# Filling the expert gate matrices by accumulating scatters into zeroed DRAM instead of one-hot products

## The chip, the core and the metric

One core of a Trainium2 chip runs the kernel. The metric is the device time of one execution in microseconds. Its engines are TensorE (PE, with its weight loads PEld), VectorE (DVE), ScalarE (ACT), GpSimd (POOL) and SyncE (SP), which here issues nearly all plain DMAs; POOL issues the indirect ones. All DMAs share 16 transfer engines.

## What is computed

A backbone of two layers over 512 latent and 256 context tokens of width 1024: gated DeltaNet in layer 0, attention in layer 1, each followed by a retrieval of experts (PEER). Everything is float32. The part that matters:

```python
def block_fn(xb):                                  # 128 tokens
    qry = (xb @ w_query).reshape(P, PEER_HEADS, 2, PEER_HALF)
    s = jnp.einsum('phcd,hckd->phck', qry, sub_keys)
    top_s, top_i = lax.top_k(s, PEER_TOPK)
    ...
    best_s, pos = lax.top_k(cand_s, PEER_TOPK)     # 16 of 256 pairs, for each of 8 heads
    idx = jnp.take_along_axis(cand_i, pos, axis=-1)   # expert 0..16383
    gate = jax.nn.softmax(best_s, axis=-1)
    act = jax.nn.gelu(jnp.einsum('pd,phkd->phk', xb, u_tab[idx]), approximate=False)
    coef = gate * act
    return jnp.einsum('phk,phkd->pd', coef, v_tab[idx])
```

So a token has 128 picks among 16384 experts, and one expert may be picked by several heads.

## The kernel before

The latents are four blocks of 128 tokens, the context two. For `ND` = 3 latent blocks the experts are evaluated densely, all 16384 for all 384 tokens; for latent block 3 and, in layer 0, for the context, the picked rows of `peer_u` and `peer_v` are gathered from DRAM by indirect DMAs, 128 rows of 4 KB each.

The dense way goes over 128 blocks of 128 experts. `act(i)` loads 512 KB of U (tile `ur`), splits it into a high and a low part (`uh` on ACT, `ul` on DVE) and makes 24 matmuls into `up` and a gelu: an act block. `mix` loads 512 KB of V (`vr`), splits it, multiplies the gelu by the gates, and makes 18 matmuls into six accumulators `y`: a mix. Some act blocks are done ahead of the dense loop, beside earlier stages, and go through DRAM (`act_d`, 192 KB each way); `tock` hands them out by the table `URATE`, as `tick` hands out steps of the gathers by `RATE`.

The mix needs the gates as a matrix [expert, token]. `gates_build` makes it after `routing`: for every token two one-hot 128x128 tiles A and B on DVE (lines 1066 and 1067), whose product on PE (`gp`, line 1068) is the token's 128x128 gate matrix; ACT copies four tokens at a time into `st` (line 1069). Five groups of 64 tokens are stored to DRAM (`G_d`, 4 MB each, line 1071) and read back 640 KB at a time in the dense loop (`gt`); the sixth stays in SBUF.

Stages, by the profile's time: dn_in and DeltaNet of context and latents; routing of layer 0 to 1950 us; gates 1950 to 2322; dense loop 2332 to 3184; attention to 3541; routing of layer 1; gates 3792 to 4105; dense loop 4112 to 4872. Block 3 is routed first, then 0, 1 and 2. The background gathers of layer 0 run through all of it: `gather_u` (line 965, a DVE product for each gathered row, line 967), `gather_v` for the context (line 1017, two matmuls on PE into `yp` for each gathered tile, line 1020) and `gather_vt` (line 981). A gather needs a free `row` buffer, and DVE or PE frees it.

A scheduler orders the instructions of each engine when the program is built; the program text sets only what depends on what. An engine runs its instructions in that order and stops at one that has to wait. On SP's and on POOL's queue each DMA also waits for the eighth one before it.

At the start SP loads the conditioning weights, then the first `dn_w_in` weights (`wr`), the tokens (`xt`, lines 288) and the modulation rows `modg`, `modS`, `modA` (one row of 4 KB spread over 128 partitions); the first normalized row (`hrow`) needs these.

Of the kernel before, what the change touches and what calls it, by code (L numbers as in the profile page):

```python
# [18 lines left out]
P = 128  # L19
# [12 lines left out]
AHEAD = [i for r in (0, 2, 1, 3) for i in range(r, PK, 4)]      # blocks of experts, in the order of their evaluation ahead  # L32


class Kern:
    def __init__(self, ctx, tc, I, out, dbg):
# [3 lines left out]
        self.ug, self.ucredit, self.nu = None, 0.0, 0  # L40
        self.cst = ctx.enter_context(tc.tile_pool(name="cst", bufs=1))
# [7 lines left out]
        nc.vector.memset(self.ones, 1.0)  # L49
        self.nhalf = c.tile([P, 64], F32, name="nhalf")  # L50
# [3 lines left out]
    # gathers are issued in small steps between the other work  # L54
# [18 lines left out]

    def drain(self, keep=0):
        while len(self.bg) > keep:
            for _ in self.bg.pop(0):
                pass
        self.credit = 0.0
# [43 lines left out]
    def ada(self, l, r, pool=None):  # L122
        """chunks 2 * r and 2 * r + 1 of a layer's modulations, for latents (row 0) and context (row 1)"""
# [24 lines left out]
    def mod_rows(self, pool, l, s, sub, norm, nb=1, pool_g=None, **kw):  # L148
        """A = norm_g*(1+scale), S = shift, as rows on all partitions"""
# [10 lines left out]
    def norm_mod(self, pool, x, A, S, h):  # L160
        """h <- rmsnorm(x) * A + S"""
# [8 lines left out]
    def transp_split(self, pp, tag, h, hi, lo, b):  # L170
        """h [128, 1024] -> hi/lo[:, kb, b*128:...]"""
# [10 lines left out]
    # tokens on the free axis: 0..511 latents, 512..767 context  # L182
    def gate_math(self, p, pp, gx, n, G):
# [23 lines left out]
        # log1p(e) = ln(u) * e / (u - 1), or e where u rounds to 1  # L207
# [30 lines left out]
    def dn_in(self, G, later, ast, rec):  # L238
        """q, k, v, z and the gates; rec's first step is traced before the last heads, beside which it runs"""
# [67 lines left out]
    def dn_qkv(self, G, p, pp, pwp, hi, lo, wtile, heads, nb):  # L307
# [4 lines left out]
        W2 = TL + 4 + TC          # conv output span: latents, gap of 4, context  # L312
        XC = TL + 6               # start of the context in the padded row
# [28 lines left out]
        for h in heads:  # L342
# [80 lines left out]
    def dn_rec(self, seq, G, og_d, st_d):  # L423
# [5 lines left out]
        with ExitStack() as st:  # L429
# [8 lines left out]
            for g0 in range(0, QH, GR):  # L438
                pks, Pss, Us = [], [], []
                pg = p if g0 // GR % 2 else pq  # L440
                for hh in range(GR):
                    h = g0 + hh
                    Ps = pg.tile([P, MH, 2, P], F32, name="Pm", bufs=GR)
                    U = pg.tile([P, MH, 2, P], F32, name="U", bufs=GR)     # (c, v), dir
# [5 lines left out]
                    for c in range(n):  # L450
# [124 lines left out]
    def dn_inv(self, p, pp, Us, MH, Z64):  # L575
        """Us[head][:, m, dir] <- (I + U)^-1, U triangular (upper for dir 0, lower for dir 1)."""
# [23 lines left out]
        R1 = t4("R1", [P, 2 * M, 32])     # rows of the inverses' transposes  # L600
        R2 = t4("R2", [P, 2 * M, 32])     # rows of the inverses
# [9 lines left out]
        # (source, target) blocks  # L611
# [56 lines left out]
    def dn_out(self, seq, og_d, xin, xout, put):  # L668
        """xout[b] = xin[b] + g1 * (o @ w_out); put(b, rows) for every finished block"""
# [33 lines left out]
    def attention(self, xl, xc, order, rows, A0, gst, ost, pst):  # L703
        """(softmax(q k^T) v)^T of the latents, split, by heads; context is read after the gathers that finish it"""
# [3 lines left out]
        with tc.tile_pool(name="att", bufs=1) as p:  # L708
# [95 lines left out]
            with tc.tile_pool(name="att3", bufs=1) as p, tc.tile_pool(name="attp", bufs=1, space=PS) as pp:  # L804
                sc = P ** -0.5
                H2 = N * P // 2
                for h in range(QH):
# [28 lines left out]
                    nc.sync.dma_start(wr, I["att_w_out"][h * P:(h + 1) * P, :])  # L836
                    self.split(wh[:, h], wl[:, h], wr)
# [24 lines left out]
    def routing(self, l, hi, lo, T, gate, idx, order, done=None):  # L862
        """gate[b], idx[b]: [128 tokens, 8 heads, 16]"""
        nc, I = self.nc, self.I
        n = T // P
        with self.tc.tile_pool(name="rt", bufs=1) as q, self.tc.tile_pool(name="rtp", bufs=1, space=PS) as pp:
# [32 lines left out]
            for b in order:  # L899
# [17 lines left out]
                for h in range(PH):  # L917
                    self.tick(self.rate[3])
                    self.tock(1)
# [34 lines left out]
                if done:  # L954
                    done(b)
# [79 lines left out]
    def gates_build(self, l, tbs, gate, idx, G_d, pk):  # L1035
# [3 lines left out]
        with tc.tile_pool(name="gb", bufs=1) as p, tc.tile_pool(name="gbp", bufs=1, space=PS) as pp:  # L1039
            iota = p.tile([P, P], F32, name="iotar")  # L1040
            nc.sync.dma_start(iota, self.I["iota128"].to_broadcast([P, P]))
            for b in tbs:
# [8 lines left out]
                for j in range(3):  # L1051
                    nc.tensor.transpose(tp[:, j], f3[:, j], self.ident)
# [390 lines left out]
```

## Time and profile before

| | |
|---|---|
| median of 3 runs | 4889.07 us (4887.17 to 4899.61) |
| the profiled execution's span | 4891.1 us |
| PE, DVE, ACT, POOL busy | 4329.9, 3587.0, 1866.5, 1321.5 us |
| DMA | 1196.55 MB, mean 245 GB/s |
| POOL's indirect DMAs | 1024 |

A row of busy time by stretch gives the stretch from the span's start, its length, the busy time of PE, PEld, DVE, ACT and POOL, each with its instructions (x), TensorE's granted clock as a share of full, the mean busy share of the 16 DMA engines and what they moved. A row in order of time gives the start, the duration, the engine (SPq is SP's queue), the line, the operation with out<-in, the count, and in brackets the engine's idle time before it and what ended it. An indirect DMA's duration on POOL is that of its issue, not of the transfer.

### The profile page before, as it was taken

Reading aid. Unit: us, or ns where it says so; the run is one execution under the profiler, and the core shown is the slowest. Engines: PE = TensorE matmul, PEld = TensorE weight load, DVE = VectorE, ACT = ScalarE, POOL = GpSimd, SP = SyncE. Lnnn points to the kernel's source line nnn. Section 1 sums busy time; section 2 is a strip of 40 time slices with the busy share of each in tenths; the row PEclk is TensorE's granted clock in tenths of the full one; section 3 lists DMA queues with packets and bytes.
Section 4 is the critical chain, followed back from the end, with each engine's and each line's share of the span. In section 5 each row is a group of like instructions: output and inputs, shape, how many; then the busy total and the mean of one; then the engine's idle time right before and its main releaser. Section 6 shows DMA issues by size and latency. Waiting matters only on the chain. (4 is left out here: it accounts for less than half of the span.)

```text
span 4891.1 us, 68996 instructions
## 1 busy us (share of the span) xinstructions
PE 4329.9 (89%) x24564; PEld 3455.1 (71%) x24564; DVE 3587.0 (73%) x8483; ACT 1866.5 (38%) x3605; POOL 1321.5 (27%) x1111
## 2 busy tenths in 40 slices
PE   6999669757569698999999999988997999999998
PEld 3778547545444556666788888745687998888887
DVE  4667825899965857566688888645579888888886
ACT  2335553447450213344333333223333554333333
POOL 0000000134344433222333334440000102444441
PEclk8999789768679899999999999999999999999999
DMA  7744246447578877777999999872133678999996
GB/s 296 261 150 135 75 144 191 153 148 254 177 242 317 301 240 268 269 260 272 329 349 351 339 339 337 292 268 74 61 112 107 215 260 287 355 334 335 336 324 230
DMA packets 480616, 1196.55 MB, mean 245 GB/s; under 512 B 40752, under 2 KB 239152, under 8 KB 470416
## 3 DMA queue, kind: packets, MB, share of 16 engines
q1 hardware_dynamic: 332816, 655.21, 38.2%
q0 software_dynamic: 147456, 536.94, 31.5%
q8 instruction: 194, 3.18, 0.3%
q14 instruction: 150, 1.23, 0.1%
HBM read 1079.50 MB, written 112.49 MB: 244 GB/s over the span
## 5 line engine op out<-in xcount | busy, mean ns | idle before, releaser
L965 POOL DMA_INDIRECT row<-in_peer_u,idx x512 | 613.2, 1198 | 1513.3 <-DVE row L967 706.3
L100 PE MATMUL up<-hil,uh 128*128 128x384 f32 x2048 | 709.4, 346 | 44.7 <-ACT c L1094 44.1
L102 PE MATMUL up<-hil,ul 128*128 128x384 f32 x2048 | 697.2, 340 | 0.0
L101 PE MATMUL up<-lol,uh 128*128 128x384 f32 x2048 | 696.1, 340 | 0.0
L100 PE MATMUL y<-vh,ch 128*128 128x512 f32 x1536 | 602.8, 393 | 9.1 <-ACT ch L106 7.6
L101 PE MATMUL y<-vl,ch 128*128 128x512 f32 x1536 | 602.9, 393 | 0.0
L102 PE MATMUL y<-vh,cl 128*128 128x512 f32 x1536 | 508.8, 391 | 0.0
L981 POOL DMA_INDIRECT row<-in_peer_v,idx x256 | 339.9, 1328 | 456.3 <-DVE lhs L984 374.5
L100 PEld LDWEIGHTS up<-hil,uh 128*128 128x128 f32 x2048 | 386.9, 189 | 94.8 <-ACT c L1094 65.4
L106 ACT CAST uh<-ur 128x1024 fp32r<-128x1024 f32 x256 | 268.3, 1048 | 454.3 <-PE up L101 322.3
L1017 POOL DMA_INDIRECT row<-in_peer_v,iT x256 | 279.5, 1092 | 557.7 <-PE yp L1020 473.7
L107 DVE TENSOR_TENSOR vl<-vr,vh 128x1024 fp32r<-128x1024 f32 x256 | 312.9, 1224 | 127.1 <-ACT vh L106 125.1
L106 ACT CAST vh<-vr 128x1024 fp32r<-128x1024 f32 x256 | 268.6, 1051 | 359.9 <-PE y L102 325.0
L101 PEld LDWEIGHTS up<-lol,uh 128*128 128x128 f32 x2048 | 387.1, 189 | 19.2 <-issue 10.9
L102 PEld LDWEIGHTS up<-hil,ul 128*128 128x128 f32 x2048 | 386.5, 189 | 18.2 <-issue 15.1
L107 DVE TENSOR_TENSOR ul<-ur,uh 128x1024 fp32r<-128x1024 f32 x256 | 312.1, 1220 | 74.7 <-ACT uh L106 70.1
L967 DVE SCALAR_TENSOR_TENSOR row<-row,ghs 128x1024 f32<-128x1024 f32 x256 | 311.2, 1222 | 73.7 <-DMA row<-in_peer_u,idx 72.7
L1066 DVE TENSOR_SCALAR A<-iotar,kt 128x128 f32<-128x128 f32 x768 | 221.8, 289 | 174.4 <-PE gp L1068 171.9
L100 PEld LDWEIGHTS y<-vh,ch 128*128 128x128 f32 x1536 | 289.8, 189 | 70.3 <-ACT ch L106 9.1
L102 PEld LDWEIGHTS y<-vh,cl 128*128 128x128 f32 x1536 | 288.6, 188 | 64.6 <-issue 4.2
L984 DVE SCALAR_TENSOR_TENSOR lhs<-row,lcf,lhs 128x1024 f32<-128x1024 f32 x254 | 325.1, 1280 | 9.6 <-DMA row<-in_peer_v,idx 8.0
L101 PEld LDWEIGHTS y<-vl,ch 128*128 128x128 f32 x1536 | 290.1, 189 | 56.3 <-issue 2.5
(397 smaller groups left out, 8788.1 us busy)
## 6 DMA issues: line engine op xcount, KB each, us to landing
ur<-in_uT SPq DMA_DIRECT2D x256, 512.0 KB
vr<-in_peer_v SPq DMA_DIRECT2D x256, 512.0 KB
w<-in_ada_w SPq DMA_DIRECT2D x48, 1024.0 KB
G_d<-st SPq DMA_DIRECT2D x10, 4096.0 KB
gt<-G_d SPq DMA_DIRECT2D x64, 640.0 KB
act_d<-c SPq DMA_DIRECT2D x129, 192.0 KB
c<-act_d SPq DMA_DIRECT2D x129, 192.0 KB
wr<-in_dn_w_in SPq DMA_DIRECT2D x48, 512.0 KB
```

Of the source, the lines that this page charges most:

```text
L100: first = mm(ps, lh, rh, start=start, stop=False)
L101: mm(ps, lh, rl, start=False, stop=False)
L102: mm(ps, ll, rh, start=False, stop=stop)
L106: self.nc.scalar.copy(hi, src)
L107: self.nc.vector.tensor_sub(lo, src, hi)
L965: nc.gpsimd.indirect_dma_start(out=u, out_offset=None, in_=self.I["peer_u"], in_offset=bass.IndirectOffsetOnAxis(ap=ix[:, k:k + 1], axis=0))
L967: mv = nc.vector.scalar_tensor_tensor(u, u, 1.0, hs, op0=ALU.mult, op1=ALU.mult, accum_out=coef[:, k:k + 1])
L981: nc.gpsimd.indirect_dma_start(out=v, out_offset=None, in_=self.I["peer_v"], in_offset=bass.IndirectOffsetOnAxis(ap=ix[:, k:k + 1], axis=0))
L984: keep(nc.vector.scalar_tensor_tensor(y, v, coef[:, k:k + 1], y, op0=ALU.mult, op1=ALU.add))
L1017: nc.gpsimd.indirect_dma_start(out=v, out_offset=None, in_=self.I["peer_v"], in_offset=bass.IndirectOffsetOnAxis(ap=iT[:, t:t + 1], axis=0))
L1066: nc.vector.tensor_scalar(A, iota, kt[:, 0, t:t + 1], None, op0=ALU.is_equal)
```

## The change

`gates_build` is gone. In its place stand six matrices in DRAM, `Gd[layer][block]`, each [16384 experts x 128 tokens], 8 MB, addressed as (j, i, token) for expert i * 128 + j. `zeros` splits each into eight pieces of 16 rows of 64 KB, and `fill` writes three of them from a DRAM row of zeros after every head of `dn_qkv` and of the attention. `places` computes each pick's address (four DVE operations for a block); `gates_place` issues for each of a block's 128 picks one indirect DMA on POOL that adds 128 gates, one for each token, into the matrix. `scat` takes a step of each block in turn, one step for each head in `routing` and the rest in `place_all`, which also calls `tick` and `tock`. The dense loop reads the gates of four expert blocks with three DMAs of 256 KB, and multiplies once instead of twice. The rates change: `RATE[0][4]` 0.88 to 0.3, `RATE[0][7]` 2.6 to 1.6, layer 0's `URATE` 0.07 and 15 to 0.2 and 2, layer 1's 0.33 to 0.23, with two small ones in layer 1.

```diff
+    def scat(self, w):
+        self.scredit += w
+        while self.scredit >= 1.0:
+            self.scredit -= 1.0
...
+            try:
+                next(self.todo[self.turn])
+                self.turn += 1
+            except StopIteration:
+                self.todo.pop(self.turn)
+
+    def fill(self, n):
+        for _ in range(min(n, len(self.fills))):
+            dst = self.fills.pop(0)
+            self.nc.sync.dma_start(dst, self.I["zero"].to_broadcast(list(dst.shape)))
...
             nc.sync.dma_start(self.pk_d[h], pk.rearrange("p a b c -> p (a b c)"))
+            self.fill(ZF)
...
-                            nc.vector.tensor_scalar(A, iota, kt[:, 0, t:t + 1], None, op0=ALU.is_equal)
-                            nc.vector.tensor_scalar(B, iota, kt[:, 1, t:t + 1], kt[:, 2, t:t + 1], op0=ALU.is_equal, op1=ALU.mult)
-                            nc.tensor.matmul(ps[:, j], B, A, start=True, stop=True)
-                        nc.scalar.copy(st[:, :, q * 4:q * 4 + 4].rearrange("p i t -> p t i"), ps)
-                    if g < G_d.shape[0]:
-                        nc.sync.dma_start(G_d[g], st.rearrange("p i t -> p (i t)"))
...
+    def gates_place(self, G, gate, at):
+
+        for k in range(PH * TOPK):
+            self.nc.gpsimd.indirect_dma_start(out=G, out_offset=bass.IndirectOffsetOnAxis(ap=at[:, k:k + 1], axis=0),
+                                              in_=gate[:, k:k + 1], in_offset=None, compute_op=ALU.add)
+            yield
...
-                nc.vector.tensor_mul(c1, c1, gt)
-                nc.vector.tensor_mul(c[:, T1:], c[:, T1:], gl[:, i])
...
+                    gt = p.tile([P, nb, GS, P], F32, name="gt", bufs=3)
+                    for b in range(nb):
+                        nc.sync.dma_start(gt[:, b].rearrange("p i t -> p (i t)"), G[b].rearrange("(j x) o -> j (x o)", j=PK)[:, i * P:(i + GS) * P])
...
+    def place_all():
+        while k.todo:
+            k.tick(k.rate[4])
+            k.tock(2)
+            k.scat(1.0)
+
+    def zeros(l):
+        k.fills += [g.rearrange("(j x) o -> j (x o)", j=PK)[j:j + 16] for g in Gd[l] for j in range(0, PK, 16)]
```

How the change moves instructions is shown at three places. The first is SP at the start, from the first `wr` loads on; this is before:

```order
L253 DMA wr<-in_dn_w_in 128x8x128 x2
L288 DMA xt<-in_x 128x1024 x2
L143 DMA ada_d_68<-row 2x512 x2
L154 DMA modg<-in_norm_g 128x1024
L143 DMA ada_d_68<-row 2x512 x2
L154 DMA modg<-in_norm_g 128x1024
L316 DMA cw<-in_convw 128x160
L146 DMA modS<-ada_d_68 128x1024 x2
L253 DMA wr<-in_dn_w_in 128x8x128
L146 DMA modA<-ada_d_68 128x1024 x2
L288 DMA xt<-in_x 128x1024 x2
L288 DMA xt<-in_ctx 128x1024 x2
```

After, eighteen fills (of the matrices numbered 85, 86 and 87, layer 0's) follow the first two `wr` loads, then two `xt` loads and the conditioning rows; the next rows there are these (88 to 90 are layer 1's matrices):

```order
L340 DMA cw<-in_convw 128x160
L277 DMA wr<-in_dn_w_in 128x8x128
L161 DMA bt<-in_ada_b 1x512 x8
L277 DMA wr<-in_dn_w_in 128x8x128
L96 DMA G_87<-in_zero 16x16384 x6
L96 DMA G_88<-in_zero 16x16384 x8
L96 DMA G_89<-in_zero 16x16384 x8
L96 DMA G_90<-in_zero 16x16384 x8
L170 DMA modS<-ada_d_70 128x1024 x2
L170 DMA modA<-ada_d_70 128x1024 x2
L312 DMA xt<-in_x 128x1024 x2
L312 DMA xt<-in_ctx 128x1024 x2
```

All 48 fills now stand ahead of the modS and modA rows and of the last four token loads.

The second is POOL in layer 0, where the gathers of the context's values end and those of `gather_u` for latent block 3 follow, beside the gates; before, with the semaphores waited for:

```order
L1017 DMA row_17463<-in_peer_v,iT_16047 128x1024 [waits DMASW3_49,PE_49]
L1017 DMA row_17489<-in_peer_v,iT_16047 128x1024 [waits DMASW4_49,PE_49]
L965 DMA row_17543<-in_peer_u,idx03_90 128x1024 [waits DMASW5_49,PE_49]
L965 DMA row_17568<-in_peer_u,idx03_90 128x1024 [waits DMASW6_49,PE_49]
L965 DMA row_17615<-in_peer_u,idx03_90 128x1024 [waits DMASW7_49,PE_49]
L965 DMA row_17640<-in_peer_u,idx03_90 128x1024 [waits DVE_49]
L965 DMA row_17665<-in_peer_u,idx03_90 128x1024 [waits DVE_49]
L965 DMA row_17690<-in_peer_u,idx03_90 128x1024 [waits DVE_49]
```

After, at the end of the same `gather_u` stretch (G00, G01 and G02 are layer 0's matrices, lg and la a block's gates and addresses):

```order
L992 DMA row_20327<-in_peer_u,idx03_97 128x1024 [waits DMASW7_49,DVE_49]
L992 DMA row_20361<-in_peer_u,idx03_97 128x1024 [waits DVE_49]
L1065 DMA G02_87<-lg2_13614,la2_13620 2097152x1 [waits DMASW3_49,DMASW1_49]
L1065 DMA G00_85<-lg0_13612,la0_13618 2097152x1 [waits DMASW5_49,DMASW2_49]
L1065 DMA G01_86<-lg1_13613,la1_13619 2097152x1 [waits DMASW6_49]
L1065 DMA G02_87<-lg2_13614,la2_13620 2097152x1 [waits DMASW4_49,DMASW1_49]
L1065 DMA G00_85<-lg0_13612,la0_13618 2097152x1 [waits DMASW2_49]
L1065 DMA G01_86<-lg1_13613,la1_13619 2097152x1 [waits DMASW3_49]
L1065 DMA G02_87<-lg2_13614,la2_13620 2097152x1 [waits DMASW7_49,DMASW4_49]
L1065 DMA G00_85<-lg0_13612,la0_13618 2097152x1 [waits DMASW5_49,DMASW0_49]
```

From there 151 scatters follow one another with no gather between, each waiting for a queue's semaphore (DMASW) of a DMA before it. In the whole of layer 0's placing POOL has 148 scatters among 116 context gathers, then 85 among 96 gathers of `gather_u`, then the 151; in layer 1 384 scatters among 91 gathers, the first 80 of them alone.

The third is PE in layer 0 up to the first mix; before:

```order
L1068 MATMUL gp<-A,B 128x128 x3
L1020 MATMUL yp<-row,Cz 32x512 x2
L1068 MATMUL gp<-A,B 128x128 x4
L1020 MATMUL yp<-row,Cz 32x512 x2
L1068 MATMUL gp<-A,B 128x128 x3
L1020 MATMUL yp<-row,Cz 32x512 x8
L100 MATMUL y_20097<-vh,ch 128x512
L101 MATMUL y_20097<-vl,ch 128x512
```

After:

```order
L124 MATMUL up<-hil,uh 128x384
L125 MATMUL up<-lol,uh 128x384
L126 MATMUL up<-hil,ul 128x384
L124 MATMUL y_20309<-vh,ch 128x512
L125 MATMUL y_20309<-vl,ch 128x512
L124 MATMUL y_20310<-vh,ch 128x512
L125 MATMUL y_20310<-vl,ch 128x512
```

The products `gp` are gone from PE; where 59 act blocks stood ahead of the first mix, 112 do now (in layer 1 73 and 124).

## Rows read from the trace of the kernel before

**Rows 1.** the page: span and part 1, busy time and instructions of each engine
```profile
span 4891.1 us, 68996 instructions
PE 4329.9 (89%) x24564; PEld 3455.1 (71%) x24564; DVE 3587.0 (73%) x8483; ACT 1866.5 (38%) x3605; POOL 1321.5 (27%) x1111
```

**Rows 2.** busy by stretch: PE, PEld, DVE, ACT, POOL; clock, DMA share, GB/s
```profile
1917.00:2332.00 415.00, 389.14 (x2163) 271.34 (x2161) 255.20 (x849) 157.47 (x185) 121.70 (x115) 0.98 0.78 271
2332.00:3184.00 852.00, 849.62 (x4062) 726.57 (x4062) 672.28 (x975) 295.03 (x396) 330.80 (x282) 1.00 0.92 334
3758.00:4112.00 354.00, 333.52 (x2135) 326.66 (x2133) 300.26 (x919) 177.80 (x221) 37.97 (x32) 1.00 0.65 227
4112.00:4872.00 760.00, 758.93 (x3622) 666.81 (x3623) 622.66 (x893) 273.49 (x366) 314.02 (x225) 1.00 0.91 327
```

**Rows 3.** groups by line, shapes: busy us, mean ns, idle before and its releasers
```profile
L1067 DVE TENSOR_SCALAR B<-iotar,kt 128x128 f32<-128x128 f32 x768 | 264.1, 344 | 0.0
...
L1068 PE MATMUL gp<-A,B 128*128 128x128 f32 x1536 | 224.5, 283 | 2.7 <-ACT st L1069 2.5
...
L1066 DVE TENSOR_SCALAR A<-iotar,kt 128x128 f32<-128x128 f32 x768 | 221.8, 289 | 174.4 <-PE gp L1068 171.9 <-PE up L102 1.3 <-PE up L101 0.4
```

**Rows 4.** PE in order of time: start, us, engine, line, operation
```profile
2041.73 1.05 PE L1020 MATMUL yp<-row,Cz 128*32 128x512 f32 x4
2042.71 1.38 PE L1068 MATMUL gp<-A,B 128*128 128x128 f32 x10
...
2046.08 0.34 PE L100 MATMUL up<-hil,uh 128*128 128x384 f32 x1
...
2047.64 0.34 PE L100 MATMUL up<-hil,uh 128*128 128x384 f32 x1
...
2601.31 0.40 PE L100 MATMUL y<-vh,ch 128*128 128x512 f32 x1
...
2604.08 1.52 PE L102 MATMUL y<-vh,cl 128*128 128x512 f32 x6
```

**Rows 5.** SP's DMA issues at the start
```profile
37.23 1.02 SPq L146 DMA_DIRECT2D modA<-ada_d  x2
...
39.67 1.28 SPq L288 DMA_DIRECT2D xt<-in_ctx  x2
```

**Rows 6.** PE at the start, in order of time
```profile
51.77 1.94 PE L176 MATMUL tr<-ident,hrow 128*128 128x128 f32 x8 [22.79 <-DVE hrow L302]
```

**Rows 7.** busy by stretch, of the start and of one gate store
```profile
27.00:60.00 33.00, 8.96 (x44) 3.82 (x44) 18.57 (x25) 11.28 (x19) 6.25 (x8) 0.52 0.91 338
...
2044.00:2068.00 24.00, 19.06 (x99) 14.17 (x99) 9.66 (x35) 6.95 (x9) 2.93 (x4) 0.86 0.94 347
```

**Rows 8.** POOL in order of time, gathers of gather_u
```profile
1275.23 0.93 POOL L965 DMA_INDIRECT row<-in_peer_u,idx  x1 [1.35 <-DVE row L967]
...
1278.95 1.18 POOL L965 DMA_INDIRECT row<-in_peer_u,idx  x1 [0.30 <-issue]
...
1481.68 0.95 POOL L965 DMA_INDIRECT row<-in_peer_u,idx  x1 [1.07 <-DVE row L967]
```

**Rows 9.** DVE in order of time, the products of two of these gathers
```profile
1280.35 1.23 DVE L967 SCALAR_TENSOR_TENSOR row<-row,ghs 128x1024 f32<-128x1024 f32 x1 [1.02 <-DMA row<-in_peer_u,idx]
...
1489.33 1.22 DVE L967 SCALAR_TENSOR_TENSOR row<-row,ghs 128x1024 f32<-128x1024 f32 x1 [0.72 <-DMA row<-in_peer_u,idx]
```

**Rows 10.** DVE: block 0's indices cast, layer 0 and layer 1
```profile
1914.70 0.22 DVE L946 CAST li<-idf 128x128 int32<-128x128 f32 x1
...
3756.86 0.22 DVE L946 CAST li<-idf 128x128 int32<-128x128 f32 x1
```

**Rows 11.** PE: the first mix of layer 0 and of layer 1
```profile
2332.45 0.80 PE L100 MATMUL y<-vh,ch 128*128 128x512 f32 x1 [1.43 <-issue]
...
4112.15 0.80 PE L100 MATMUL y<-vh,ch 128*128 128x512 f32 x1 [6.50 <-ACT ch L106]
```

**Rows 12.** SP: one plain DMA issue
```profile
2044.80 0.32 SPq L1071 DMA_DIRECT2D G_d<-st  x1
```

More of the change, by code (lines that the diff above doesn't have):

```diff
@@ L954, in routing @@
                 if done:
-                    done(b)
+                    done(q, b)
     def gather_u(self, l, p, hs, gate, idx, coef):
@@ L1099, in act_ahead, with dense @@
         self.nc.sync.dma_start(self.act_d[i], c)
-    def dense(self, G_d, gl, xin, put, rp=None):
+    def dense(self, G, xin, put, rp=None):
         nc, tc, I = self.nc, self.tc, self.I
@@ L1250, in body @@
     k.act_d = dr("act_d", [PK, P, ND * P])
-    G_d = dr("G_d", [ND * 2 - 1, P, PK * 64])
+    Gd = [[dr(f"G{l}{b}", [PK * PK * P, 1]) for b in range(ND)] for l in range(2)]
     pers = ctx.enter_context(tc.tile_pool(name="pers", bufs=1))
@@ L1258, in picks, with place @@
         p = st.enter_context(tc.tile_pool(name="lgi", bufs=1, side="right"))
-        return [{b: p.tile([P, PH, TOPK], t, name=f"{nm}{b}") for b in range(ND)} | of(d, 0) for d, nm, t in ((gate, "lg", F32), (idx, "li", I32))]
+        lat = [{b: p.tile([P, PH, TOPK], t, name=f"{nm}{b}") for b in range(ND)} | of(d, 0) for d, nm, t in ((gate, "lg", F32), (idx, "li", I32))]
+        return lat, {b: p.tile([P, P], I32, name=f"la{b}") for b in range(ND)}
+    def place(l, q, b, lat, at):
+        k.places(q, lat[1][b], at[b])
+        k.todo.append(k.gates_place(Gd[l][b], lat[0][b].rearrange("p h k -> p (h k)"), at[b]))
+    def place_all():
[5 more added lines that the diff above has]
+        k.fills += [g.rearrange("(j x) o -> j (x o)", j=PK)[j:j + 16] for g in Gd[l] for j in range(0, PK, 16)]
     of = lambda d, s: {b: v for (q, b), v in d.items() if q == s}
@@ L1274, in body @@
         rec = k.dn_rec("c", G, og_c, st_d)
+        zeros(0)
         k.dn_in(G, [k.ada(l, r) for l in range(2) for r in range(3) if l or r], st, rec)
@@ L1314, in body, with gathers @@
         vctx(i // 2, i % 2)
-    def gathers(b):
-        if b >= ND:
+    def gathers(q, b):
+        if b < ND:
+            place(0, q, b, lat, at)
+        else:
             j = NX + b - ND
@@ L1332, in put @@
         fresh.pop(b - 2, None)
-    gl = k.gates_build(0, range(ND), *lat, G_d, lst.enter_context(tc.tile_pool(name="gk", bufs=1)))
+    place_all()
     k.tock(3)
@@ L1339, in body @@
     A0 = k.mod_rows(ap, 1, 0, 0, "norm1_g", pool_g=k.up, tag="raw", bufs=3)
-    k.dense(G_d, gl, xm_l, put, ap)
+    k.dense(Gd[0], xm_l, put, ap)
     lst.close()
@@ L1353, in body @@
     k.drain(2 * NX - NVA)
+    zeros(1)
     k.attention(xo_l, xo_c, [*range(ND, NL), *range(1, ND), 0], fresh, A0, gst, ost, pst)
@@ L1371, in body, with gathers @@
     k.dense_open(lst, 1, ND, hi, lo)
-    def gathers(b):
-        if b >= ND:
+    def gathers(q, b):
+        if b < ND:
+            place(1, q, b, lat, at)
+        else:
             gat.u(1, b - ND, gate[0, b], idx[0, b])
             gat.v(b - ND, idx[0, b], (1, 0, 5), rows(xm2, b), lambda y: put(b, y))
-    lat = picks(gst)
+    lat, at = picks(gst)
     k.routing(1, hi, lo, TL, *lat, order, gathers)
-    gl = k.gates_build(1, range(ND), *lat, G_d, lst.enter_context(tc.tile_pool(name="gk", bufs=1)))
+    place_all()
     k.tock(3)
-    k.dense(G_d, gl, xm2, put)
+    k.dense(Gd[1], xm2, put)
     k.drain()
```

69 lines of the change are left out of this document (26 added, 43 removed).

## The prediction

> **What bounds the kernel now.** I read the page first, then busy time by stage, then PE's, POOL's and SP's order of time in the stages that the change touches. Sums are made against the profiled execution, 4891 us [rows 1], 2 us over the median of the three runs. PE is busy for 89% of it. The two gate stages and the two dense stages fill it almost wholly [rows 2]: from layer 0's first ready indices to its first mix PE works 389 of 415 us, in layer 1 334 of 354; in the dense stages 850 of 852 and 759 of 760, beside DMA at 0.92 and 0.91 of its time and 334 and 327 GB/s. So DVE's one-hot products (222 and 264 us for both layers, 225 us of PE with them [rows 3]) do not stand in the way by themselves: act blocks fill the gaps beside them. What the change can win is PE's share of the products, about 225 us, and only if PE has other work throughout.
>
> PE's prices: nine `up` matmuls start in 1.56 us, so an act block of 24 is 4.2 us; twelve `y` matmuls in 2.77, so a mix of 18 is 4.15; one gathered context value is 0.98 [rows 4]. Layer 1's dense stage confirms it: 55 acts and 128 mixes are 231 + 531 = 762 us against 760.
>
> **Part 1: the zeros.** 48 fills of 1,048,576 bytes are 50.3 MB, DRAM to DRAM. The code writes three per head of dn_in and of the attention; but nothing holds them, and in SP's order all 48, layer 1's too, stand between the first two `wr` loads and the modS, modA, x and ctx loads. In the trace these are issued at 37 and 40 us [rows 5], and PE's first transpose, which had waited 22.8 us for the normalized row, comes at 51.8 [rows 6]. All of dn_in is behind that, so the fills' whole time lies on the path. Nothing hides it: the stretch from 27 to 60 us already has DMA at 0.91 and 338 GB/s [rows 7]. No row shows a DRAM to DRAM copy. From below: a stretch with a 4 MB store to DRAM moves 347 GB/s [rows 7], so 145 us. From above: each byte is read from DRAM and written to it, which no row has; both counted at 347 GB/s give 290 us. A gain is excluded, since nothing was there before. No row is nearer to one end, so I take the middle: **+217**. The fills' source is one row read over and over; the rows of [rows 7] hold such broadcast loads and are not slow, so I add nothing for that. The Trainium skill (DMA: Bandwidth & Descriptors, Latency and other measured facts) gives copies between HBM tensors 207 GB/s at a row pitch of 512 KiB and 103 at 4 MiB; an estimate from the first is 243 us, and the sum would be 5536. No run here shows such a copy.
>
> **Part 2: placing in layer 0.** 384 scatters of 128 elements replace the products. Each goes to one of three matrices and waits until the one before it on the same matrix has landed; POOL issues in order, so behind a waiting scatter stand the gathers, behind these DVE's row products, and behind those DVE's `ul` splits, on which PE's act blocks wait. I call three scatters, one per matrix, a round. A POOL issue takes 0.93 to 0.95 us and 0.30 more to the next [rows 8], so I take 1.25 per DMA, a scatter's 128 descriptors like a gather's. How long a scatter takes to land no row shows. The nearest row is a gather: issued at 1275.23, its DVE product starts at 1280.35, a wait that the row ended: 5.1 us; in a saturated stretch it is 1481.68 to 1489.33, 7.65 [rows 8, 9]. A scatter moves almost nothing, but reads DRAM before it writes there. Ends: 3.75 us a round (POOL's own three issues) and 7.5; I take 5.0 beside act blocks, next to the 5.1, and 4.5 where acts have run out. The Trainium skill (DMA: Bandwidth & Descriptors, Anatomy of one DMA) gives a fixed 2.0 us plus bytes over 436 GB/s. By that the gather would be 0.93 + 3.2 = 4.1 us, where the row shows 5.1; a round would fall to POOL's three issues, which is the first rival below.
>
> Block 0's indices are cast at 1914.7 [rows 10]; with the address arithmetic the first scatter stands at 1917 in the old clock. POOL's order has three stretches. (a) 148 scatters among 116 context gathers: POOL 264 x 1.25 = 330; PE's order has 52 acts there, 52 x 4.2 + 116 x 0.98 = 332. Each waits for the other at times: 340. (b) 85 scatters among 96 gathers for `gather_u`: 181 x 1.25 = 226, PE's 38 acts (160) beside them. (c) 151 scatters with nothing between, 53 rounds with the last matrix's lag: 53 x 4.5 = 239; PE has done the 112 acts that its order puts ahead of the first mix, and idles. Sum 805. SP's `gt` loads wait for the last scatters too, and all later `vr` and `ur` loads are queued behind them. 8 us for that load put the first mix at 2730, 398 later than 2332 [rows 11].
>
> In return, 16 acts instead of 69 are left. PE: 16 x 4.2 + 128 x 4.15 + 37 context values x 0.98 = 634 us. But DMA has V 67.1 MB, U 8.4, stored acts 22.0, gates 25.2 and 197 gathers 103.3, together 226 MB; at 340 GB/s, between the dense stages' 334 and the 347, that is 664, which decides. The stage ends at 3394 against 3184: **+210**. That 15 of the context values leave the attention's start I count at nothing (at most 15 us). The fewer DVE instructions of a mix (one product instead of two) lie under it too.
>
> **Part 3: placing in layer 1.** First scatter at 3757 [rows 10]. Twelve scatters go to matrix 0 before matrix 2's first, so the last chain ends after about 139 rounds. With 91 gathers among 384 scatters POOL's own issues are 475 x 1.25 = 594; 139 rounds of 5.0 are 695, and the waits decide. PE's 107 acts (449) fit beside. First mix at 3757 + 695 + 8 = 4460 instead of 4112 [rows 11]. Then 4 acts and 128 mixes are 548 us of PE, but V 67.1, U 2.1, acts 24.4, gates 25.2 and 165 gathers 86.5 MB are 205 MB, 604 us at 340 GB/s. End 5064, and the 19 us from 4872 to the span's end as before: 5083, **+192**.
>
> Sum: 4891 + 217 + 210 + 192 = **5510**. Setting up addresses (four small DVE operations a block) and the removed 4 MB stores (42 MB, against 50 MB of gate loads and 50 of zeros) are inside the stages above.
>
> **Rivals.** *The scatter lands fast*, and POOL's three issues set a round. For it: it carries 512 bytes; against: the 5.1 us. (a) 340, (b) 226, (c) 53 x 3.75 = 199: first mix 2690, end 3354, +170. Layer 1: 594, end 4982, +91. With the same fills **5369**.
>
> *The scatter lands slowly*, 7.5 us, as gathers in a saturated stretch do, because each element is read before it is written and shares its queue with gathers. (a) 49 rounds 368, (b) 28 rounds 230, (c) 53 x 7.5 = 398: first mix 2921, end 3585, +401; layer 1: 139 x 7.5 = 1043, end 5431, +540. **6049**.
>
> *PE alone sets the pace from the first scatter to the last mix* (the other side). Place: both placings and dense stages. Layer 0 then takes 332 + 160 + 8 + 634 us and ends at 3051, -133; layer 1 takes 449 + 8 + 548 and ends at 4781, -110; with the fills **4865**. It decides from a round of 3.2 us among layer 1's gathers (449 / 139) and of 0.5 us in stretch (c) ((4891 - 4865) / 53), so from scatters that cost POOL less than the 0.32 us that a plain issue costs SP [rows 12], against 0.93 [rows 8]; and DMA would have to carry 205 MB in 548 us, 374 GB/s, where no stretch shows over 347.
>
> That the change does not do what it says holds for the fills alone: they are not early beside other work but ahead of it, as costed.
>
> **How the numbers follow.** Forecast 0.50, fast landing 0.24, slow landing 0.20, PE's pace 0.04, something else between 0.02. The predicted time is the forecast's, 5510. With fills at 145 the fast case is 5297, and DMA some per cent faster takes it to 5180; with fills at 290 the forecast is 5583, and landings between 5.0 and 7.5 reach 6000. The range 5180 to 6000 leaves out PE's pace, the end of the fast case and the upper half of the slow one, about 2 in 10. A measurement of this kernel tells 0.3% from no change. Faster by more needs PE's pace: 0.04. Within 0.3%: 0.02. Slower: 0.94.
>
> **What would show it.** Part 1: PE idle and DMA near full from about 30 to 245 us, then dn_in as before; wrong if the stretch is under 100 us or other work stands in it. Part 2: PE idle in layer 0 for some 240 us before its first mix while POOL issues nothing but scatters, each wait ended by the scatter before on its matrix; wrong if PE stays busy there. Part 3: rounds of about 5 us on POOL in layer 1, `y` starting some 350 us after the old 4112 plus the shift already gathered. Dense: DMA over 0.9 busy and PE below 0.95. The forecast falls if scatters land in under 4 us or over 6, or if a scatter's own POOL time is far from 0.95.

## The result, and the profile after

The changed kernel takes **5993.9 us** (median of 4 runs, 5991.4 to 5999.3) beside 4891.2 for the kernel before on the same chip (4887.2 to 4899.6): a ratio of 1.225, 95% interval 1.2235 to 1.2269. That is inside the range, at its upper edge, and 484 us above the forecast of 5510.

The page of the profiled execution, its span, part 1 and three rows of the slices (each slice 150 us), answering to [rows 1]:

```profile
span 5997.5 us, 65797 instructions
PE 4324.0 (72%) x23010; PEld 3373.9 (56%) x23010; DVE 3216.6 (54%) x6691; ACT 1661.2 (28%) x3407; POOL 2580.0 (43%) x1879
PE   0599769575679987767007999988974655559998
POOL 0000000143453378888884344300038888843332
PEclk5799889676789998898558999989997787879999
```

PE lost its products and is still busy for 4.3 ms: the granted clock of the whole execution fell from 0.933 to 0.862 of full, and the matmuls into `up` of one line take 375 ns on average instead of 346. POOL's busy time nearly doubled. PE is at zero in the slices 1, 20 and 21, and where POOL stands at 8, PE stands at 4 to 7 or at 0.

Busy time by stretch, answering to [rows 2, 7] (PE, PEld, DVE, ACT, POOL, granted clock, DMA share, GB/s): the fills, the three parts of layer 0 (placing beside other work, scatters alone, dense), then layer 1 (placing, the time to the first mix, dense).

```profile
60.00:120.00 60.00, 0.00 (x0) 0.00 (x0) 0.24 (x1) 0.00 (x0) 0.00 (x0) 0.50 0.95 300
...
2103.00:2895.00 792.00, 573.10 (x2658) 434.96 (x2656) 243.68 (x309) 132.29 (x183) 649.80 (x452) 0.88 0.81 231
2895.00:3168.00 273.00, 0.00 (x0) 0.00 (x0) 0.00 (x0) 0.00 (x0) 224.32 (x146) 0.50 0.25 6
3182.00:3846.00 664.00, 646.33 (x2860) 502.71 (x2860) 491.25 (x604) 211.98 (x289) 262.77 (x205) 1.00 0.94 342
...
4408.00:5327.00 919.00, 512.35 (x2323) 468.18 (x2323) 243.49 (x303) 139.19 (x194) 736.94 (x476) 0.81 0.59 128
5327.00:5403.00 76.00, 46.83 (x230) 43.63 (x228) 23.10 (x28) 15.51 (x22) 12.31 (x12) 0.88 0.69 231
5403.00:5981.00 578.00, 548.92 (x2400) 448.99 (x2400) 468.38 (x578) 193.19 (x264) 205.01 (x154) 1.00 0.92 340
```

POOL's busy time does not hold the 0.30 us between two issues. With it POOL is full: 650 + 452 x 0.30 = 785 of 792 us, and 737 + 476 x 0.30 = 880 of 919. It is the bound of both placings. Its instructions in order of time, first where scatters run alone in layer 0, then beside gathers in layer 1, answering to [rows 8]:

```profile
2962.29 1.55 POOL L1065 DMA_INDIRECT G<-lg,la  x1 [0.30 <-issue]
2964.15 1.55 POOL L1065 DMA_INDIRECT G<-lg,la  x1 [0.30 <-issue]
2966.01 1.55 POOL L1065 DMA_INDIRECT G<-lg,la  x1 [0.30 <-issue]
...
4804.19 1.55 POOL L1065 DMA_INDIRECT G<-lg,la  x1 [0.30 <-issue]
4806.05 0.99 POOL L992 DMA_INDIRECT row<-in_peer_u,idx  x1 [0.30 <-issue]
4807.35 1.58 POOL L1065 DMA_INDIRECT G<-lg,la  x1 [0.30 <-issue]
...
4840.45 1.98 POOL L1065 DMA_INDIRECT G<-lg,la  x1 [0.30 <-issue]
```

A scatter's issue is 1.55 us, not the gather's 0.95, and the idle time before it ends by the issue itself, not by an earlier scatter. Three scatters, one per matrix, are 5.57 us, longer than a landing (a median of 3.4 us, shown further on), so the landing is mostly hidden. The scatters of layer 1's placing as a group (busy, mean ns, idle before, and what ended it), then its last scatter, and PE's first mix in layer 0 and in layer 1:

```profile
L1065 POOL DMA_INDIRECT G<-lg,la x383 | 637.7, 1665 | 372.8 <-DVE idf L972 221.1 <-issue 108.1 <-DMA G<-lg,la 43.7
...
5324.30 1.57 POOL L1065 DMA_INDIRECT G<-lg,la  x1 [1.76 <-DMA G<-lg,la]
...
3182.48 0.79 PE L124 MATMUL y<-vh,ch 128*128 128x512 f32 x1 [325.31 <-ACT ch L130]
...
5403.45 0.79 PE L124 MATMUL y<-vh,ch 128*128 128x512 f32 x1 [6.10 <-ACT ch L130]
```

Waits for an earlier scatter are 44 us there (the 221 us stand before the first one). From the last scatter to the first mix it is 79 us in layer 1 and 15 in layer 0.

Where the 1106 us between the two profiled executions (4891.1 and 5997.5) come from, cut at the cast of block 0's indices and at the dense stages' ends:

| stretch | before | after | difference | forecast |
|---|---|---|---|---|
| start to layer 0's indices | 1914.7 | 2095.2 | +180 | +217 |
| indices to the end of dense, layer 0 | 1266.5 | 1750.2 | +484 | +210 |
| attention and routing | 575.7 | 554.2 | -21 | 0 |
| layer 1's indices to the end | 1134.2 | 1597.9 | +464 | +192 |

### The profile page after: what moved, and what is told of

It reads as the page before. It is cut to its first block, busy times and chain, and to the rows that moved or that the text cites. A ratio compares the mean times of both kernels' runs of the same rounds, so it can differ in the third digit from the quotient of the medians.

```text
span 5997.5 us, 65797 instructions
## 1 busy us (share of the span) xinstructions
PE 4324.0 (72%) x23010; PEld 3373.9 (56%) x23010; DVE 3216.6 (54%) x6691; ACT 1661.2 (28%) x3407; POOL 2580.0 (43%) x1879
## 3 DMA queue, kind: packets, MB, share of 16 engines
q14 instruction: 152, 1.25, 0.1%
## 5 line engine op out<-in xcount | busy, mean ns | idle before, releaser
L1065 POOL DMA_INDIRECT G<-lg,la x768 | 1275.9, 1661 | 497.8 <-DVE idf L972 221.1
L124 PE MATMUL up<-hil,uh 128*128 128x384 f32 x2048 | 767.6, 375 | 280.5 <-ACT c L1099 280.3
L126 PE MATMUL up<-hil,ul 128*128 128x384 f32 x2048 | 752.5, 367 | 278.1 <-DVE ul L131 278.1
L125 PE MATMUL up<-lol,uh 128*128 128x384 f32 x2048 | 740.7, 362 | 0.0
L124 PE MATMUL y<-vh,ch 128*128 128x512 f32 x1536 | 459.1, 395 | 373.2 <-ACT ch L130 335.0
L994 DVE SCALAR_TENSOR_TENSOR row<-row,lhs 128x1024 f32<-128x1024 f32 x256 | 311.6, 1224 | 751.2 <-DMA row<-in_peer_u,idx 750.4
L126 PEld LDWEIGHTS up<-hil,ul 128*128 128x128 f32 x2048 | 427.3, 209 | 312.9 <-DVE ul L131 297.2
L126 PE MATMUL y<-vh,cl 128*128 128x512 f32 x1536 | 562.3, 390 | 0.0
L130 ACT CAST ch<-c 128x384 fp32r<-128x384 f32 x256 | 130.8, 513 | 903.4 <-DVE c L1122 402.5
L1047 PE MATMUL yp<-row,Cz 128*32 128x512 f32 x1024 | 258.7, 638 | 95.7 <-DMA row<-in_peer_v,iT 95.7
```

The source lines that it names most:

```text
L124: first = mm(ps, lh, rh, start=start, stop=False)
L125: mm(ps, lh, rl, start=False, stop=False)
L126: mm(ps, ll, rh, start=False, stop=stop)
L130: self.nc.scalar.copy(hi, src)
L994: mv = nc.vector.scalar_tensor_tensor(u, u, 1.0, hs, op0=ALU.mult, op1=ALU.mult, accum_out=coef[:, k:k + 1])
L1047: nc.tensor.matmul(yp[sl(2 * g + j), :], Cz[:, (32 * g + i) * 32:(32 * g + i + 1) * 32], v[:, j * 512:(j + 1) * 512], start=i == 0, stop=i ...
```

## The experiments

Theory 1, formed on the trace of after: the fills cost what they delay, and POOL's issue of an adding scatter (1.56 + 0.30 us) sets the pace of both placings. Its rival is the prediction's own reason, that the wait for the landing of the scatter before on the same matrix sets the pace. A time with no ratio beside it is that of one execution.

**e1: the fills held to their place.**

```diff
-            self.nc.sync.dma_start(dst, self.I["zero"].to_broadcast(list(dst.shape)))
+            self.tc.keep_in_program_order(self.nc.sync.dma_start(dst, self.I["zero"].to_broadcast(list(dst.shape))))
```

> The changed kernel, with each head's three zero fills held to their place in the program, so that layer 0's stand beside dn_in and layer 1's beside the attention. Theory 1 (the fills lie on the path only because they stand ahead of everything): the first transpose of the normalized row comes near 55 us instead of 222, layer 0's block 0 indices near 1925 to 1960 instead of 2095, layer 1's stage as long as before; total 5994 - 171 = 5823, up to 5860 if dn_in gives some of it back. Rival (50 MB of DMA cost the same wherever they stand, since the stages beside them are near their DMA limit too): 5950 to 6000.

Measured 5818.8 us, ratio 1.189 (1.187 to 1.192): 175 less. The first transpose of a normalized row, in the changed kernel and then in e1 (PE in order of time; the bracket is its idle time before):

```profile
222.51 1.73 PE L200 MATMUL tr<-ident,hrow 128*128 128x128 f32 x7 [193.12 <-DVE hrow L326]
```

```profile
52.93 1.30 PE L200 MATMUL tr<-ident,hrow 128*128 128x128 f32 x5 [23.20 <-DVE hrow L326]
```

Busy time of e1 in dn_in, columns as above:

```profile
60.00:400.00 340.00, 337.00 (x2147) 264.95 (x2147) 233.42 (x292) 113.64 (x184) 19.70 (x7) 1.00 0.76 263
```

The fills now raise the DMA share of dn_in to 0.76 (0.59 in the kernel before) while PE stays busy for 337 of 340 us. Ahead of the work the bytes cost 175 us more than beside it. What they still cost there is at most small: layer 0's indices come at 1928.8 us, 14 later than in the kernel before, and no run tells the fills' share of that from the new rates'. That settles where part 1's time comes from.

**e2: one chain by the order of the program.** The step to the next block in `scat` was taken out.

```diff
                 next(self.todo[self.turn])
-                self.turn += 1
```

> The changed kernel, with the scatters of one block all placed before those of the next, so that each scatter waits for the one just ahead of it (one chain in place of three). Theory 1 (with three chains POOL's issue, 1.56 + 0.30 us a scatter, sets the pace, and landings of 3.0 to 4.5 us are hidden): now the landing shows, about 3.4 us a scatter where nothing else runs and 4.3 beside gathers; layer 0's placing grows from 1079 to about 1500 us, layer 1's from 916 to about 1650, total near 7100. Rival (the prediction's own: the wait for the scatter before on the same matrix already sets three scatters' pace): three times the placing, layer 1 near 2750, total above 9000.

Measured 5982.6, as the changed kernel. It tells nothing about the two theories: where scatters run alone they still follow each other at 1.86 us, less than a link of one chain takes (3.3 us, e6 below), so three chains ran as before, whatever the order of the program text. e6 makes the same test in a way that the order can't undo.

**e6: one chain by one tensor.**

```diff
-    Gd = [[dr(f"G{l}{b}", [PK * PK * P, 1]) for b in range(ND)] for l in range(2)]
+    Gw = [dr(f"G{l}", [ND * PK * PK * P, 1]) for l in range(2)]
...
+        if b:
+            nc.vector.tensor_scalar(at, at, b << 21, None, op0=ALU.bitwise_or)
```

> The changed kernel, with a layer's three matrices made one tensor (the block's number goes into the address), so that every scatter waits for the landing of the one before it: one chain in place of three. The order on POOL stays. Theory 1: a link takes 3.76 us where nothing else runs, as in the series of e4, and 4.2 to 4.5 beside gathers; layer 0's 151 alone take 568 us instead of 281, its 233 others about 1000 instead of 792, layer 1's 384 1460 to 1730 instead of 916: 7000 to 7350. Rival (three chains were already paced by their landings, a round of 5.6 us being one landing and its wait): a link of 5.6 us, placing of 2100 us a layer, above 8000.

Measured 7055.6. POOL where the scatters run alone, and the scatters of the whole run as a group:

```profile
3301.10 1.55 POOL L1065 DMA_INDIRECT G<-lg,la  x1 [1.67 <-DMA G<-lg,la]
3304.34 1.55 POOL L1065 DMA_INDIRECT G<-lg,la  x1 [1.69 <-DMA G<-lg,la]
...
L1065 POOL DMA_INDIRECT G<-lg,la x768 | 1241.0, 1616 | 1536.6 <-DMA G<-lg,la 1286.6
```

Now each scatter does wait for the one before it, 1287 us in all, and a link is 3.3 us; in layer 1 384 scatters with 103 gathers among them take 1512 us, 3.9 a scatter. The order on POOL, which had been expected to stay, changed: 307 scatters, not 151, run alone in layer 0, in 1013 us, so what this run shows is the link and the waits, not the total. With three chains both 3.3 and 3.9 are well under the 5.57 us in which POOL comes back to the same matrix. The rival's 8000 falls, and with it the prediction's reason.

**e4: seven kinds of indirect DMA in a row**, behind the last output.

```diff
+    for f in (add4, put4, get4, add512, put4k, add4k, get4k):
+        f()
```

> The changed kernel, and behind its last output seven series of twelve indirect DMAs each on POOL: add 4 bytes, write 4 bytes, gather 4 bytes, add 512 bytes, write 4 KB, add 4 KB, gather 4 KB for each of 128 partitions, the writes in one chain. Theory 1 (the accumulation makes the issue dear): 1.56 us for the three that add, 0.95 for the others. Rival (a scatter is dear because of its direction, to DRAM, or of its element of 4 bytes): 1.56 for every write, or for every 4-byte form. Landing: the chain's period with 4 bytes about 3.3 us if a scatter lands in 3.0, added or not; above 5 if the add is a read and a write one after the other and the plain write is faster. Total about 6270.

One row of each series on POOL, in that order:

```profile
6004.61 1.54 POOL L1437 DMA_INDIRECT G<-prx,pra  x1 [2.23 <-issue]
...
6041.53 0.96 POOL L1441 DMA_INDIRECT G<-prx,pra  x1 [1.46 <-DMA G<-prx,pra]
...
6064.70 0.94 POOL L1445 DMA_INDIRECT prv<-G,pra  x1 [0.30 <-issue]
...
6093.32 1.54 POOL L1449 DMA_INDIRECT G<-prx,pra  x1 [2.42 <-DMA G<-prx,pra]
...
6142.58 0.95 POOL L1453 DMA_INDIRECT G<-prx,pra  x1 [2.62 <-DMA G<-prx,pra]
...
6210.34 1.54 POOL L1457 DMA_INDIRECT G<-prx,pra  x1 [4.90 <-DMA G<-prx,pra]
...
6253.31 0.94 POOL L1461 DMA_INDIRECT pru<-G,pra  x1 [0.34 <-DMA pru<-G,pra]
```

The issue is 1.54 us for the three that add (4 bytes, 512 bytes, 4 KB for each partition) and 0.94 to 0.96 for the four that don't, to DRAM or from it. So it is the adding that is dear for POOL, not the direction or the size. From issue to issue in its chain an add of 4 bytes takes 3.8 us and a plain write 2.4, so the plain write lands sooner too.

**e5: plain writes in place of adds.**

```diff
-                                              in_=gate[:, k:k + 1], in_offset=None, compute_op=ALU.add)
+                                              in_=gate[:, k:k + 1], in_offset=None)
```

> The changed kernel, with scatters that write instead of adding; where two heads of a token pick the same expert, only one of the gates is left. Theory 1 (POOL's issue of a scatter, 1.56 + 0.30 us, sets the placing's pace; a plain one is 0.96 + 0.30): layer 0's 151 scatters alone take 191 us instead of 281, the 233 beside gathers 140 less, layer 1's placing 230 less: 5994 - 90 - 140 - 230 = 5535, up to 5570 where PE's act blocks begin to decide. Rival (the landing beside other traffic decides, 4 us and more whatever the kind): no more than half of that, above 5760.

Measured 5625.7: 368 less, four fifths of the 461 us of issue time that the edit takes from POOL, so between the two, nearer to theory 1. Layer 0's time from its first scatter to its first mix is 872 us instead of 1079, layer 1's 824 instead of 995. The edit shortens the landing as well as the issue (e4), so e5 alone does not tell one from the other; e6 does. What is missing in layer 1 are waits for landings, which the shorter issues no longer hide: POOL is busy for 512 + 475 x 0.30 = 654 of 750 us, and of the rest 113 us (44 in the changed kernel) are waits for an earlier scatter. The scatters of that stretch as a group:

```profile
L1065 POOL DMA_INDIRECT G<-lg,la x384 | 409.3, 1066 | 429.5 <-DVE idf L972 221.2 <-DMA G<-lg,la 112.7 <-issue 95.6
```

**e12: the same scatter for fewer partitions.**

```diff
+    for n, add in ((P, 1), (64, 1), (32, 1), (P, 0), (64, 0), (32, 0)):
+        put(n, add)
```

> The changed kernel, and behind its last output six series of ten scatters of 4 bytes each, in one chain: adds for 128, 64 and 32 partitions, then plain writes for 128, 64 and 32. Theory 1 (the issue is mostly work for each address, twice as much of it where the scatter adds): from 1.54 and 0.96 us the issue falls by half of the difference of both for 64 partitions, to about 1.0 and 0.7, so that a scatter for half a block costs about two thirds. Rival (the issue is a price per DMA, adding included): 1.54 and 0.96 whatever the partitions. Total near 6180.

POOL, adds for 128, 64 and 32 partitions, then a plain write for 32:

```profile
6019.02 1.54 POOL L1439 DMA_INDIRECT G<-prx,pra  x1 [2.19 <-issue]
...
6045.45 1.42 POOL L1439 DMA_INDIRECT G<-prx,pra  x1 [1.62 <-DMA G<-prx,pra]
...
6080.90 1.33 POOL L1439 DMA_INDIRECT G<-prx,pra  x1 [1.67 <-DMA G<-prx,pra]
...
6147.95 0.86 POOL L1441 DMA_INDIRECT G<-prx,pra  x1 [1.35 <-DMA G<-prx,pra]
```

The rival holds nearly: a quarter of the addresses still costs 1.33 of 1.54 us. It is mostly a price per DMA, so smaller scatters save little each, and more of them would be needed.

**e3, e7, e9: the 79 us from layer 1's last scatter to its first mix.** e3 issues the gate loads from POOL's queue, e7 takes the gathers out of layer 1's placing, e9 does both.

```diff
-                        nc.sync.dma_start(gt[:, b].rearrange(
+                        nc.gpsimd.dma_start(gt[:, b].rearrange(
...
-[0, 0, 0, 0, 0.26, 2.6, 0, 1.3, 6.25, 0, 0])
+[0, 0, 0, 0, 0, 2.6, 0, 1.3, 6.25, 0, 0])
```

> The changed kernel, with the loads of the gates (gt) issued from POOL's queue instead of SP's. Theory 1 (in layer 1 the loads that wait for the last scatters hold up the U loads queued behind them, so act blocks are still left when placing ends): the 79 us from the last scatter to the first mix of layer 1 fall to 20 to 35, layer 0's 15 us stay; total 5994 - 50 = 5940, less 0 to 10 that POOL's 192 more issues cost in the dense stages. Rival (the acts are late because POOL's gathers and DVE are late, whatever SP does): 5994, within 10 us, or later by POOL's issues.

> The changed kernel, with no gathers of latent block 3 beside the placing of layer 1 (they all come in the dense stage). Theory 1 (the act blocks are late because their splits stand behind row products on DVE, whose gathers stand behind scatters on POOL): 384 scatters at 1.86 are 714 us, acts run freely beside them, first mix 4408 + 714 + 20 = 5142 instead of 5403; the dense stage carries 91 more gathers, 47.7 MB or 140 us at 340 GB/s: total 5994 - 261 + 140 = 5873. Rival (act blocks are late by their own loop or by SP's queue, as the 5.8 us of a block alone suggest): the first mix still 60 us or more behind the last scatter.

> As e7 (no gathers beside layer 1's placing), and the gate loads (gt) on POOL's queue as in e3, so that both ties are cut: no row products ahead of the splits on DVE, no gate loads that wait ahead of the U loads on SP. Theory 1: in e7 PE stood idle from 4800 to 5150 us because SP waited with a gate load for the last scatters, and 29 act blocks were left; now they all run beside the scatters at 5.8 us each (107 in 620 us), the first mix comes 10 to 30 us behind the last scatter, near 5170 instead of 5339: 6100 - 170 = 5930. Rival (the blocks stop for another reason, such as the buffers of the stored acts): first mix still near 5340.

e3 measured 5980.8 (ratio 1.223, 1.221 to 1.225), 13 less, which the intervals do not tell from the changed kernel's, with the first mix still 63 us behind the last scatter: SP's queue alone was not it. In layer 1's placing the changed kernel has these groups on PE and DVE (busy, mean ns, idle before, and what ended it):

```profile
L124 PE MATMUL up<-hil,uh 128*128 128x384 f32 x770 | 298.3, 387 | 168.7 <-ACT c L1099 168.7
L126 PE MATMUL up<-hil,ul 128*128 128x384 f32 x771 | 295.6, 383 | 236.6 <-DVE ul L131 236.5
...
L994 DVE SCALAR_TENSOR_TENSOR row<-row,lhs 128x1024 f32<-128x1024 f32 x91 | 111.4, 1225 | 586.8 <-DMA row<-in_peer_u,idx 586.8
```

PE waits 237 us for the splits `ul`; these stand on DVE behind row products, which wait 587 us for gathers, which stand on POOL behind scatters. e7 cuts that tie, and runs into the other. SP in e7:

```profile
4813.00 0.33 SPq L1091 DMA_DIRECT2D ur<-in_uT  x1
5114.63 1.28 SPq L1137 DMA_DIRECT2D gt<-G  x3
```

For 302 us SP waits with a gate load for a matrix's last scatter, U loads behind it. PE does 153 us of act blocks in each 200 us up to 4800, then 27 us in the next 200, and blocks are left over: first mix 176 us behind the last scatter. It measured 6100.4 where 5873 was expected, dearer than the changed kernel: gathers of block 3 now run on for 189 us behind the last mix, with PE nearly idle. e9 cuts both and measured 5968.7: PE works evenly until its blocks are done at 5045, and the first mix comes 15 us behind the last scatter, 196 us earlier than in the changed kernel. Of that only 25 us reach the end, since 193 us of gathers stand behind the last mix here too.

```profile
4800.00:5000.00 200.00, 26.67 (x144) 24.76 (x144) 7.35 (x6) 7.69 (x12) 167.41 (x108) 0.59 0.26 11
```

```profile
4800.00:5000.00 200.00, 154.17 (x828) 143.22 (x826) 42.12 (x35) 48.77 (x68) 168.87 (x103) 1.00 0.58 125
```

(the same stretch in e7 and in e9). So the 79 us were act blocks held back in two queues at once, and removing one tie leaves the other.

**e8: what it would bring if placing were free.** Fills as in e1, and no scatters.

```diff
-        for k in range(PH * TOPK):
+        for k in range(0):
```

> The changed kernel with its fills held to their place (as e1), and no scatter at all: the gates stay zero, so what is left is all but the placing. Theory 1 (the placing alone costs what e1 leaves over; with it gone PE and DMA set the pace): layer 0's first mix near 1938 + 500, its end 664 later at 3102, attention 543, layer 1's first mix 457 after its indices, dense 577: 4700 to 4760, some 150 us under the kernel before, the most that leaving the products could bring at these rates. Rival (the new rates and the heavier dense stages eat the gain themselves): 4850 to 4900.

Measured 4753.0, 135 less than the kernel before beside it. So leaving out the products and the stores of their results, with the fills in place, is worth 135 us at these rates, and the placing by 768 scatters costs 1066 (5819 of e1 less 4753).

**e10, e11: one block of one layer.** The kernel before, with block 0 of layer 1 alone placed by scatters.

```diff
+            k.todo.append(k.gates_place(G0, lat[0][0].rearrange("p h k -> p (h k)"), at))
...
-    gl = k.gates_build(1, range(ND), *lat,
+    gl = k.gates_build(1, range(1, ND), *lat,
```

> The kernel before, with only latent block 0 of layer 1 placed by scatters (one matrix, its eight fills held beside the attention's heads, its gate loads on POOL's queue), blocks 1 and 2 by one-hot products, and more act blocks and gathers beside them (123 acts ahead instead of 72). Theory 1: one chain of 128 links of 3.8 to 4.3 us is 490 to 550 us, first mix near 4290 instead of 4112; PE is spared 37 us of products and fills the rest with act blocks that the dense stage then lacks: dense 531 to 560 us, total 4850 to 4900 against 4889. Rival (act blocks alone take 5.8 us, so PE does not fill the stretch, or the chain is slowed by the gathers between): first mix 4350 or later, 4930 and above.

> As e10, with the gate loads on SP's queue and 104 act blocks ahead instead of 123. Theory 1: the gate loads hold SP until the chain ends, with act blocks behind them: first mix later than in e10 by the blocks left, 5.8 us each, and a dense stage longer by 24 - 5 blocks of 4.2 us: 4900 to 4990. Rival (SP is not held, since the chain ends before the other blocks' products): 4870 to 4900 as e10.

e10 measured 5071.3 (ratio 1.037, 1.035 to 1.039), e11 5110.9 (1.045, 1.043 to 1.047). The scatters of e10 as a group:

```profile
L94 POOL DMA_INDIRECT G<-lg,la x128 | 219.4, 1714 | 500.6 <-DMA G<-lg,la 266.4 <-DVE idf L980 223.6 <-issue 10.6
```

With a single matrix the landing shows: 266 us of waits, 128 scatters in 647 us (5.1 a link, with gathers and other traffic between), first mix at 4473 instead of 4112. That is e10's rival case. e11 lies above both of its cases: its chain took 629 us, its first mix came at 4458, and its dense stage took 634 us instead of e10's 565. To save 37 us of products the stretch has to hold 128 scatters one after the other. No version here that places all the gates beats the kernel before.

## Why the prediction came out as it did

**Part 1 was right in mechanism, and its term too large**: +180 against 217. PE stands still and DMA is near full, as foretold, at 300 GB/s with each byte counted once: 50.3 MB in 168 us. The bound with each byte counted twice (290 us) is refuted. The copy rates that the prediction quoted from the Trainium skill (DMA: Bandwidth & Descriptors, Latency and other measured facts) gave an estimate of 243 us. They stand there for tiles with a row pitch of 512 KiB and more, and each of these fills writes 1 MB without a gap; the trace shows 300 GB/s for them, so here the measurement decides.

**Parts 2 and 3 failed at one step: "a scatter's 128 descriptors like a gather's", 1.25 us of POOL.** The adding issue is 1.55 + 0.30, so that POOL's issues set the pace, where the sum let the waits for landings decide in (c) and in layer 1. The 1.25 was also that of a gather with nothing beside it: [rows 8] hold one of 1.18 + 0.30, and the 512 gathers of that line took 1.20 + 0.30 on average. The landing, on which the sum put the weight, was over-estimated: 5.0 us to the next scatter on a matrix taken, 3.3 measured in e6. Two errors of opposite sign: the round of three came out at 5.57 against 5.0 and 4.5, for another reason. Both signs that the prediction gave for its own fall came true: landings under 4 us, and a POOL time of a scatter far from 0.95. The row of the scatters in the list of DMA issues (the last number is the median from issue to landing, us):

```profile
G<-lg,la POOLq DMA_INDIRECT x768, 3.4
```

The estimate from the Trainium skill's fixed 2.0 us plus bytes (DMA: Bandwidth & Descriptors, Anatomy of one DMA) led to the fast-landing rival, in which POOL's issues set the round. The traces agree that they set it. That rival's 5369 had the wrong issue in it; the slow rival's 6049 is nearest to the time and has the wrong mechanism. (Its 230 us for 28 rounds of 7.5 is a slip: the rounds are 210, POOL's own issues 226.) That the time still lies in the range, 6 us under its end, is luck: that end was reached with fills of 290 us and landings of 5.0 to 7.5.

The sum redone with the measured issue: (a) 148 x 1.86 + 116 x 1.25 = 420, (b) 85 x 1.86 + 96 x 1.25 = 278, (c) 151 x 1.86 = 281, where 792 and 272 were measured (146 of the 151 in the second); layer 1 384 x 1.86 + 91 x 1.25 = 828 against 916. What is left, 94 in layer 0 and 88 in layer 1, is mostly longer issues: over 1.56 us the scatters took 38 us more in layer 0 and 40 in layer 1, over 0.95 the gathers 37 and 10. In layer 1 the waits for landings are another 44. Sorted by what DVE does in the first 1.5 us of an issue, the 496 scatters beside no DVE work take 1.57 us on average, 73 beside a `ul` split 1.79, 90 beside a row product 1.71, and 94 beside both 2.00; the mean of all is 1.66. The Trainium skill (GPSIMD Engine Reference, Specifications) says that POOL's SBUF interfaces are shared with DVE and contended by DVE instructions with two SBUF inputs; the split and the row product are such instructions, and for these the trace agrees. So do the gathers of the kernel before: 72 beside the one-hot products A and B, which read one full tile and a column, take 0.96 us, as those beside no DVE work (0.95), and 54 beside a row product 1.36. It is not the whole account, since 13 beside nothing but the short product `c`, which reads two tiles, stay at 0.95.

**"8 us for that load" was too small in layer 1**: 79, by the two ties above. The prediction named both queues (POOL's gathers with DVE behind, SP's `gt` loads with `ur` behind) and priced what they hold back at nothing. In e6, whose act blocks are done before the last scatter, layer 1's first mix comes 9 us behind it.

**"An act block of 24 is 4.2 us" holds only beside other work.** Alone it is 5.8: `up` has one buffer, and ACT does the next `uh` cast, 1.04 us, ahead of the gelu that frees it (read from the order; no run moved the cast). ACT in the changed kernel, once the scatters are over:

```profile
5359.45 1.04 ACT L130 CAST uh<-ur 128x1024 fp32r<-128x1024 f32 x1 [4.34 <-PE up L125]
5360.40 0.48 ACT L1099 ACTIVATE c<-up 128x384 f32<-128x384 f32 x1
5365.23 1.04 ACT L130 CAST uh<-ur 128x1024 fp32r<-128x1024 f32 x1 [4.34 <-PE up L125]
```

Before, products and context values filled these gaps ([rows 4]). In the changed kernel POOL's pace hid most of it; it shows in e9 (PE busy for 154 of 200 us) and e10.

**Right**: PE idle in layer 0 while nothing but scatters is issued (240 us foretold, 325 measured up to the first mix), the length of the dense stages and their DMA rates (forecast 664 and 604 at 340 GB/s, measured 663 and 577 at 342 and 340), and PE's pace out of reach. That DMA decides in the dense stages is not shown: PE was to be busy for less than 0.95 of them, and was for 646 of 664 us in layer 0 (0.97) and 549 of 578 in layer 1 (0.95), so both are near their limit. The attention's gain of 21 us had been put at nothing, and no run tells its cause.

## What to carry to other kernels

An indirect DMA that adds costs its issuing engine 1.86 us here however little it moves, so replacing arithmetic by scatters is priced by their number: 128 scatters for a block are 238 us of POOL, against 37 us of PE for its products, with DVE's part of them beside PE's other work. Measure the issue of the exact form (adding or plain) and ask what stands behind it in the same queue, and what stands behind that on the next engine. And look at the order that the scheduler makes, not at the program text: here the fills, which nothing held, were put ahead of the loads that all the work waits for, and one line that held them brought 175 us.

## What the runs showed of the hardware

- Adding raises the issue of an indirect DMA from 0.96 to 1.54 us, the same for 4 bytes, 512 bytes and 4 KB each; from 128 to 32 partitions it falls only to 1.33, a plain one to 0.86 (e4, e12).
- In one chain, from issue to the next issue: 2.4 us for plain writes of 4 bytes, 3.3 (e6) to 3.8 (e4, always the same addresses) for adds, 3.6 for plain writes and 6.6 for adds of 4 KB rows (e4).
- Beside DVE's splits and row products, which read two tiles, the issue of an adding scatter rose from 1.57 us to between 1.71 and 2.00 on average, and beside row products that of a gather from 0.95 to 1.36; beside the one-hot products, which read one, a gather's was 0.96.
- A DRAM to DRAM fill from one broadcast row into pieces of 1 MB ran at 300 GB/s.
